# One order for the recurrence: a hand-written order on five engines, second buffers, pair sums between chain steps, and loads in another order

## The chip, the cores and the metric

The kernel runs on one core of one Trainium2 chip. The time is device microseconds (us) of one execution, as the median of several runs. The engines are PE (TensorE matmul, its weight loads shown as PEld), DVE (VectorE), ACT (ScalarE), POOL (GpSimd) and SP (SyncE, which here only issues DMAs).

## The reference, cut to what matters

A two-layer trunk for 1024 tokens of width 1024, in float32. Layer 1 mixes tokens with a gated linear recurrence (HGRN2, 8 heads of 128), layer 2 with windowed attention; each layer ends with a gated feed-forward part. The change lies in the first mixer and in what is loaded and prepared beside it:

```python
q, f, i, g = split(h @ w_in, 4)                # 1024 x 4096 weights, 8 heads of 128
fg = lb + (1 - lb) * sigmoid(f)                # the decay, per token and channel
# S_t = diag(fg_t) S_{t-1} + (1 - fg_t) i_t^T ;  o_t = S_t^T silu(q_t), in chunks
o = hgrn2_chunkwise(silu(q), 1 - fg, i, log(fg))
o = o * rsqrt(mean(o^2) + eps) * g_norm_w * silu(g)
mix = o @ w_out
h = layer_norm(ALPHA * h + mix)                # then the feed-forward part, layer 2, ...
```

## The kernel before, in words

**Matmuls in three products.** Each large product is done with both operands split in a high and a low part: ACT casts the high part, DVE subtracts to get the low part (`split_raw`, `split`: ACT line L151 or L196, DVE line L144), and PE does three matmuls for each pair of tiles (`mm3`, lines L169, L170, L171). Weights arrive in three `raw` buffers (`raw_tail`) and are split into a ring `HL` of six tiles.

**The recurrence stage**, about the first 515 us, walks heads 0 to 7 in *slots*, stretches of projection matmuls. Each head has four slots of `qf` (f and q projections by halves of 512 tokens; ACT makes sigmoid, `fg`, and `kp` = 1 − fg; DVE multiplies `qs`) and four slots of `ig_block` (value and gate projections of two token blocks; ACT writes `V` at L684 and `G` at L685, DVE multiplies `G` at L686). Around each slot, `slot_begin` issues loads and stores on SP and `slot_end` makes the weight splits for the next head and, in some slots, four *pair sums* (L999 to L1002): differences of quarter blocks of the second feed-forward weights, which are loaded into the free tiles of `Y`, summed and stored to memory for later.

**The chain** of a head is the task `recur(h)`. It is spawned at slot `lead[h]` of the `ig_block` slots (lead 3 for head 1, 2 for heads 2 to 5, 1 for heads 6 and 7) and interleaved with the slots' matmuls: every `yield n` lets about n us of other matmuls go first, counted by modelled matmul costs in `od.t`. Its steps, for one head:

- DVE: `r0` (tile `St`, L858), `qp` (L859), `r1` (tile `kd`, L861), `update(0)` (qp L848, kp L850, tot L853), and two products `r2` (tile `og`, L865). This is called the r-chain below.
- PE: column sums of r0, r1, r2 (L175, `psax<-St,one`, `<-kd,one`, `<-og,one`), then `update(1)` (qp and tot on DVE, kp on POOL) and four masked copies into `Ab` (L828).
- for i = 2 to 6: PE `scores` (`psax<-qp,kp`), then `update(i)` and a copy: each step's scores need the previous step's `update`.
- PE transposes, ACT copies `kd`; then state products, `St` on DVE, output products, `og`, and at the end transposes of `og`.

**Who sets the order.** In before only PE and SP have the source's order in this stage (`manual_schedule` with PE and SP). On ACT, DVE and POOL a scheduler places each instruction where its own costs say, with the splits and the pair sums held behind two anchors (`issue_after`). After head 7 the output projection begins (`out_part`), which needs `T` filled from `Y` (`Y_to_T`, lines L196 and L144) and `w_out` loaded and split. Convolution parameters (`conv_params`) are loaded by ACT's DMA queue, transposed on PE (L769), late in this stage.

Of the kernel before, what the change touches and what calls it, by code (L numbers as in the profile page):

```python
# [87 lines left out]
def trunk(ctx: ExitStack, tc: tile.TileContext, a: dict, out: bass.AP):  # L88
# [574 lines left out]
    with tc.tile_pool(name="t", bufs=1, reuse_waits="tile") as raws, hgrn_pool as hp:  # L663
# [9 lines left out]

        VG = {}

        def ig_block(h, us, tp):
            if tp == 0:
                VG[h] = (hp.tile([P, NB, P], F32, name="V"), hp.tile([P, NB, P], F32, name="G"))
            V, G = VG[h]
            ps = psmm()  # L680
            proj_tok(us, tp, ps)
            pv = ps.rearrange("p (t g c) -> p t g c", t=2, g=2)
            ts = slice(2 * tp, 2 * tp + 2)
            nc.scalar.copy(V[:, ts, :], pv[:, :, 0, :])  # L684
            act = nc.scalar.activation(G[:, ts, :], pv[:, :, 1, :], AF.Sigmoid)  # L685
            return act, nc.vector.tensor_tensor(G[:, ts, :], G[:, ts, :], pv[:, :, 1, :], op=ALU.mult)  # L686
# [10 lines left out]
        with tc.tile_pool(name="ep", bufs=1, reuse_waits="tile") as ep:  # L697
            pr = ep.tile([81, P], F32, name="pr")

            def x_load(tb):  # L700
                nc.sync.dma_start(Y[:, tb, :], x[tb * P:(tb + 1) * P, :])

            def x_block(tb):
                ps = psax()
                for kc in range(KC):
                    tr(ps[:, kc * P:(kc + 1) * P], Y[:, tb, kc * P:(kc + 1) * P])
                ts = slice(tb * P, (tb + 1) * P)
                split(T[:, 0, :, ts], T[:, 1, :, ts], ps.rearrange("p (k t) -> p k t", k=KC))
# [8 lines left out]
            nc.scalar.copy(warm, nhalf)  # L717
            with tc.manual_schedule(engines={EN.PE, EN.SP, EN.Activation, EN.DVE}):
                x_load(0)
# [21 lines left out]
            mf = hp.tile([P, 7 * BL + P], F32, name="kd")  # L741
            nc.sync.dma_start(mf, a["masks"])
# [12 lines left out]
            nc.vector.tensor_tensor(lbt[:, 0, :], le[:, 0, :], lm, op=ALU.mult)  # L755
            nc.vector.tensor_scalar(lbt[:, 1, :], lbt[:, 0, :], -1.0, 1.0, op0=ALU.mult, op1=ALU.add)
            ig_block(0, us, NB // 2 - 1)

        def conv_params():
            yield 360.0  # L760
            for l in range(2):
                for k in range(2):
                    cr = hp.tile([88, P], F32, name="cr", bufs=2)
                    for j in range(2):
                        q = 2 * k + j
                        src = a["ffn_conv_w"][l, q] if q < 3 else a["ffn_conv_b"][l]
                        nc.scalar.dma_start(cr[44 * j:44 * (j + 1), :], src.rearrange("(c p) -> c p", p=P))
# [4 lines left out]
                    yield 0.0  # L772
# [5 lines left out]
            yield 0.0  # L778
# [3 lines left out]
            nc.vector.tensor_copy(rl, ps[:16, :2 * P])  # L782
            nc.scalar.dma_start(rbd, rl.unsqueeze(1).to_broadcast([16, P, 2 * P]))

        params = od.spawn(conv_params())

        def qf_load(h, g):
            wv = w_in.rearrange("(kc p) c -> p kc c", p=P)
            c0 = g * D + h * P
            return load(lambda r: [(r.rearrange("p (k c) -> p k c", k=KC), wv[:, :, c0:c0 + P])])  # L790

        def qf_split(raw):
            return split_raw(raw).rearrange("p h (k c) -> p h k c", k=KC)

        def qf(h, weights):
# [3 lines left out]
            kp = hp.tile([P, S], F32, name="kp")  # L799
            for half in range(2):  # L800
# [4 lines left out]
                act = nc.scalar.activation(fg[:, ts], fg[:, ts], AF.Identity, bias=lbt[:, 0, h:h + 1],  # L805
                                           scale=lbt[:, 1, h:h + 1])
                nc.scalar.activation(kp[:, ts], fg[:, ts], AF.Identity, bias=one[:, 0:1], scale=-1.0)
                yield act, None
                ps = psmm()
                proj_T(weights["q"], half, ps)  # L810
                act = nc.scalar.activation(qs[:, ts], ps, AF.Sigmoid)
                yield act, nc.vector.tensor_tensor(qs[:, ts], qs[:, ts], ps, op=ALU.mult)
            weights["out"] = qs, fg, kp

        def recur(h, qs, fg, kp):
# [65 lines left out]
            for i in range(2, 7):  # L881
# [19 lines left out]
                put()  # L901
                if i == 4:
# [60 lines left out]
        busy = {s for c in begins for s in (c, c + 1)}  # L963
        free, loads, sums, stores = {r: 0 for r in (0, 2, 4, 6)}, {}, {}, {}
        for i in range(2 * pairs):
            for s in range(8 * NH):
                for r in free:
                    at = next(n for n in range(s + 2, 9 * NH) if n not in busy and n not in sums)
                    if s not in loads and free[r] <= s and at + 1 <= begins[r] + 4:
                        break  # L970
# [3 lines left out]
            loads[s], sums[at], stores[at + 1], free[r] = (i, r), (i, r), (i, r), at + 2  # L974
        slot_no = [-1]
        anchor = {}

        def slot_begin():
# [5 lines left out]
            if n in loads:  # L984
                i, r = loads[n]
                for k in range(2):
                    row = (k * pairs + i % pairs) * P
                    nc.sync.dma_start(Y[:, r + k, :], a["ffn_w_out"][i // pairs][row:row + P, :])

        def slot_end(act, dve, *makes):  # L990
            anchor["act"], anchor["dve"] = act, dve or anchor.get("dve", act)
            with tc.issue_after(anchor["act"].ins), tc.issue_after(anchor["dve"].ins):
                for make in makes:
                    make()
                if slot_no[0] in sums:
                    r = sums[slot_no[0]][1]
                    blocks = Y[:, r:r + 2, :].rearrange("p a (b n) -> p a b n", b=2)
                    (b11, b12), (b21, b22) = [(blocks[:, k, 0], blocks[:, k, 1]) for k in range(2)]
                    tt(b11, b12, b11, op=sub)  # L999
                    tt(b12, b22, b12, op=sub)  # L1000
                    tt(b22, b22, b11, op=sub)
                    tt(b21, b21, b22, op=sub)  # L1002

        values_done = [-1]
        with tc.manual_schedule(engines={EN.PE, EN.SP}):
            w = {g: qf_split(qf_load(0, k)) for k, g in enumerate("qf")}
# [3 lines left out]
            for k in range(4):  # L1010
                slot_begin()
                slot_end(*next(steps), *(make_w[k - 1:k] if k else ()))
# [4 lines left out]
            for h in range(1, NH):  # L1017
# [4 lines left out]
                for make in ((), make_ig[:1], make_ig[1:], ()):  # L1022
                    slot_begin()
                    slot_end(*next(steps), *make)
# [5 lines left out]
                else:  # L1030
                    make_w = []
                for tp in range(NB // 2):
# [4 lines left out]
                    slot_end(*ig_block(h, us, tp), *(make_w[tp - 1:tp] if tp else ()))  # L1037
                w = nw
        od.finish([params])
        wo = a["hgrn_w_out"][0]  # L1040
        rows1 = lambda k: [(0, P, wo[k * P:(k + 1) * P, :])]
# [3 lines left out]
        us = []  # L1045
        for u in range(4):
            us += out_unit(rows1, u)
# [345 lines left out]
```

## Time and profile before

| | us |
|---|---|
| median of 3 runs | 2214.83 (2211.97 to 2215.96) |
| profiled execution, its own time | 2211.82 |
| its span, first to last instruction | 2209.8 |
| outside the span | 2.0 |
| mean granted PE clock | 0.997 |
| recurrence stage within the span | about 0 to 515 |

Of the span PE is busy 98%, DVE 80%, ACT 42%, POOL 8%. A row of a timeline reads: start, duration, engine, line, operation, output tile <- input tiles, shape, count; in brackets the idle time of the engine before it and what ended that. A row of the windows view lists a stretch, its length, busy time of each engine with instruction counts, the granted clock, the busy share of the DMA engines and GB/s. A row of the waits view lists the engine, the line that waited and for what, the total wait, how often, and the longest wait.

### The profile page before, as it was taken

The numbers are of one execution on the slowest core, as the hardware profiler recorded it, in microseconds if no ns is written. First come the engines' busy times: TensorE is split into PE (matmuls) and PEld (weight loads), VectorE is DVE, ScalarE is ACT, GpSimd is POOL, SyncE is SP. The second block draws the span as 40 slices with busy tenths as digits, with TensorE's granted clock in tenths as the row PEclk, the third lists the DMA queues.
The fourth block names the chain that finished last, engine by engine and source line by source line (L and its number), as shares of the span: only waits on it lengthen the run. The fifth ranks groups of instructions, "written<-read, shape, count | busy, mean of one in ns | idle before, by whom it ended". The sixth has DMA issues, their size and how long they took to land.

```text
span 2209.8 us, 33157 instructions
## 1 busy us (share of the span) xinstructions
PE 2168.1 (98%) x13007; PEld 1810.5 (82%) x13007; DVE 1777.6 (80%) x2415; ACT 932.1 (42%) x1601; POOL 178.6 (8%) x196
## 2 busy tenths in 40 slices
PE   8999999989999999999999999999999999999998
PEld 7888888878888888887888888878888888887887
DVE  2777665555789888988997779977899888889987
ACT  4333333332744334344343546655654444343431
POOL 0122111110100000000000013211000000000001
PEclk9999999999999999999999999999999999999999
DMA  6565443152223222227954431123123222249663
GB/s 197 173 208 195 161 168 120 48 97 89 96 69 104 86 86 86 86 79 252 303 162 153 106 99 35 34 81 120 67 96 105 80 73 77 86 153 315 202 208 137
DMA packets 231942, 281.14 MB, mean 127 GB/s; under 512 B 29977, under 2 KB 160746, under 8 KB 228970
## 3 DMA queue, kind: packets, MB, share of 16 engines
q1 hardware_dynamic: 228898, 276.57, 38.6%
q10 hardware_dynamic: 2888, 2.45, 0.9%
q8 instruction: 102, 1.67, 0.3%
q14 instruction: 54, 0.44, 0.1%
HBM read 213.96 MB, written 65.01 MB: 126 GB/s over the span
## 4 chain that ended last, share of the span: by engine, by line
PE 82%; DVE 9%; DMA 4%; ACT 3%; issue 2%; POOL 1%; SPq 0%; DVEq 0%; ACTq 0%; POOLq 0%
PE psmm L169 17%; PE psmm L171 17%; PE psmm L170 16%; PE psax L171 8%; PE psax L169 8%; PE psax L170 8%; PE psax L175 3%; DVE T L144 1%; PE psmm L175 1%; PE psax L1185 1%; PE psax L179 1%; DVE HL L144 1%; ACT Y L244 1%; DMA raw<-in_hgrn_w_out_dram 1%; DMA raw<-in_hgrn_w_in_dram 1%
## 5 line engine op out<-in xcount | busy, mean ns | idle before, releaser
L169 PE MATMUL psmm<-T,HL 128*128 128x512 f32 x768 | 307.1, 400 | 0.0
L170 PE MATMUL psmm<-T,HL 128*128 128x512 f32 x768 | 300.2, 391 | 2.1 <-DVE T L144 2.1
L171 PE MATMUL psmm<-T,HL 128*128 128x512 f32 x768 | 300.8, 392 | 0.0
L474 DVE SCALAR_TENSOR_TENSOR Y<-Y,cwt 128x1023 f32<-128x1023 f32 (+1 forms) x176 | 225.3, 1280 | 39.9 <-ACT Y L472 39.7
L472 ACT ACTIVATE Y<-Y,cwt 128x1024 f32<-128x1024 f32 x88 | 109.1, 1240 | 263.6 <-DVE Y L461 260.6
L169 PE MATMUL psmm<-HL,T 128*128 128x256 f32 (+1 forms) x656 | 201.0, 306 | 1.0 <-ACT T L196 1.0
L171 PE MATMUL psmm<-HL,T 128*128 128x256 f32 (+1 forms) x656 | 196.2, 299 | 2.0 <-DVE T L144 2.0
L170 PE MATMUL psmm<-HL,T 128*128 128x256 f32 (+1 forms) x656 | 196.3, 299 | 1.7 <-DVE HL L144 1.7
L196 ACT CAST HL<-rx 128x1024 fp32r<-128x1024 f32 (+1 forms) x137 | 140.3, 1045 | 122.4 <-DMA rx<-in_ffn_w_in_dram 33.3
L144 DVE TENSOR_TENSOR HL<-rx,HL 128x1024 fp32r<-128x1024 f32 (+1 forms) x137 | 165.9, 1213 | 12.3 <-ACT HL L196 12.0
L170 PEld LDWEIGHTS psmm<-T,HL 128*128 128x128 f32 x768 | 144.4, 188 | 31.3 <-DVE T L144 2.9
L169 PEld LDWEIGHTS psmm<-T,HL 128*128 128x128 f32 x768 | 144.3, 188 | 31.1 <-issue 1.2
L171 PEld LDWEIGHTS psmm<-T,HL 128*128 128x128 f32 x768 | 144.1, 188 | 31.0
L171 PE MATMUL psax<-T,HL 128*128 128x512 f32 x352 | 137.6, 391 | 0.0
L169 PE MATMUL psax<-T,HL 128*128 128x512 f32 x352 | 137.5, 391 | 0.0
L170 PE MATMUL psax<-T,HL 128*128 128x512 f32 x352 | 137.4, 390 | 0.0
L169 PEld LDWEIGHTS psmm<-HL,T 128*128 128x128 f32 x656 | 127.4, 194 | 7.8 <-issue 2.9
L171 PEld LDWEIGHTS psmm<-HL,T 128*128 128x128 f32 x656 | 127.2, 194 | 5.9 <-DVE T L144 2.7
L170 PEld LDWEIGHTS psmm<-HL,T 128*128 128x128 f32 x656 | 127.5, 194 | 5.4 <-DVE HL L144 2.1
L218 POOL TENSOR_TENSOR rs<-rs,nhalf 128x1 f32<-128x1 f32 x32 | 26.0, 813 | 1293.2 <-DVE rs L217 1292.9
L850 POOL TENSOR_TENSOR kp<-kp,tot 128x512 f32<-128x512 f32 x48 | 73.6, 1534 | 293.6 <-PE psax L175 151.7
L196 ACT CAST HT<-rx 128x1024 fp32r<-128x1024 f32 (+1 forms) x51 | 44.0, 863 | 89.4 <-PE psmm L170 30.5
(298 smaller groups left out, 5251.5 us busy)
## 6 DMA issues: line engine op xcount, KB each, us to landing
rx<-in_ffn_w_in_dram SPq DMA_DIRECT2D x136, 256.0 KB, 3.4
rx<-gd SPq DMA_DIRECT2D x118, 256.0 KB, 3.5
Y<-in_ffn_w_out_dram SPq DMA_DIRECT2D x44, 512.0 KB, 6.6
bsd<-Y SPq DMA_DIRECT2D x22, 1024.0 KB, 3.9
gd<-Y SPq DMA_DIRECT2D x44, 512.0 KB, 2.7
rx<-in_ffn_w_out_dram SPq DMA_DIRECT2D x54, 256.0 KB, 3.8
R<-bsd SPq DMA_DIRECT2D x44, 256.0 KB, 4.8
Y<-in_ffn_w_in_dram SPq DMA_DIRECT2D x40, 256.0 KB, 3.3
```

What stands on the lines that cost most here:

```text
L144: make = lambda e: e.tensor_tensor(lo, src, hi.bitcast(F32), op=ALU.subtract)
L169: nc.tensor.matmul(ps, st(0), mv(0), start=start, stop=False)
L170: nc.tensor.matmul(ps, st(0), mv(1), start=False, stop=False)
L171: nc.tensor.matmul(ps, st(1), mv(0), start=False, stop=stop)
L175: nc.tensor.matmul(ps, lhsT, rhs, start=start, stop=stop, **kw)
L179: nc.tensor.transpose(ps, src, ident)
L196: nc.scalar.copy(hi, src)
L218: nc.gpsimd.tensor_tensor(rs, rs, nhalf, op=ALU.pow)
L244: nc.scalar.activation(hf[:, kc, :], ps[:, k * P:(k + 1) * P], AF.Identity, bias=shift, scale=scale)
L472: nc.scalar.activation(c, u, AF.Identity, bias=cwt[:, l, 3, ci:ci + 1], scale=cwt[:, l, 2, ci:ci + 1])
L474: nc.vector.scalar_tensor_tensor(c[:, sh:], u[:, :S - sh], cwt[:, l, 2 - sh, ci:ci + 1], c[:, sh:], op0=ALU.mult, op1=ALU.add)
L850: (nc.gpsimd if i else nc.vector).tensor_tensor(kv[:, :, 0, :], kv[:, :, 0, :], tv[:, :, 1:2].to_broadcast([P, nb, m]), op=ALU.mult)
```

## The change

Line numbers of the kernel after are some 7 to 14 higher than before's in this part (L848 becomes L856, L865 becomes L873; the pair sums, L999 to L1002, all become L1013).

- `V`, `G` and `kp` get two buffers each. In `ig_block` the sigmoid now comes before the copy of `V`.
- The recurrence runs with the source's order on PE, SP, ACT, DVE and POOL. The anchors go; the splits stand at the end of a slot as written.
- The pair sums are put in a list in `slot_begin`, and taken from it by `between(n)`: four at a slot's end, two after each score step, four after the values. The slot kept free of them is one before the chain's first slot instead of the two after it. The store comes two slots after the sums instead of one.
- The largest score step (i = 6) uses blocks of 32 columns of `kp` instead of 64.
- Loads at the start: tokens 4 and 5, f weights, tokens 6 and 7, q weights, parameters, masks; before: parameters, tokens 4 to 7, masks, q, f. Convolution parameters are loaded ten units of matmul time ahead of their transposes.
- At the end of the stage three of the four `w_out` units are loaded at head 7 and split at the ends of its slots 1 to 3, instead of after all slots.

```diff
-                VG[h] = (hp.tile([P, NB, P], F32, name="V"), hp.tile([P, NB, P], F32, name="G"))
+                VG[h] = (hp.tile([P, NB, P], F32, name="V", bufs=2), hp.tile([P, NB, P], F32, name="G", bufs=2))
...
+            nc.scalar.activation(G[:, ts, :], pv[:, :, 1, :], AF.Sigmoid)
             nc.scalar.copy(V[:, ts, :], pv[:, :, 0, :])
-            act = nc.scalar.activation(G[:, ts, :], pv[:, :, 1, :], AF.Sigmoid)
-            return act, nc.vector.tensor_tensor(G[:, ts, :], G[:, ts, :], pv[:, :, 1, :], op=ALU.mult)
+            nc.vector.tensor_tensor(G[:, ts, :], G[:, ts, :], pv[:, :, 1, :], op=ALU.mult)
...
+                for tb in range(4, 6):
+                    x_load(tb)
+                rawf = qf_load(0, 1)
+                for tb in range(6, NB):
+                    x_load(tb)
+                rawq = qf_load(0, 0)
...
-                for tb in range(4, NB):
-                    x_load(tb)
+                nc.sync.dma_start(mf, a["masks"])
...
-            kp = hp.tile([P, S], F32, name="kp")
+            kp = hp.tile([P, S], F32, name="kp", bufs=2)
...
                         for b in range(P // (2 * m)):
-                            o = 2 * m * b
-                            mm32(ps[o:o + m, c * P + o + m:c * P + o + 2 * m],
-                                 kp[:, c * P + o:c * P + o + m],
-                                 qp[:, c * P + o + m:c * P + o + 2 * m], cost=0.056 * m / 32,
-                                 tile_position=(0, o))
+                            t = c * P + 2 * m * b + m
+                            for o in range(2 * m * b, 2 * m * b + m, BL):
+                                mm32(ps[o:o + BL, t:t + m], kp[:, c * P + o:c * P + o + BL], qp[:, t:t + m],
+                                     cost=0.03 * m / BL, tile_position=(0, o))
...
                 update(i)
                 put()
+                between(2)
...
             nc.vector.tensor_tensor(og, pv, G, op=ALU.mult)
+            values_done[0] = h
+            between(4)
+            yield 5.0
             nc.vector.tensor_tensor(og, og, ss.unsqueeze(2).to_broadcast([P, NB, P]), op=ALU.mult)
-            values_done[0] = h
-            yield 8.0
+            yield 3.0
...
-        busy = {s for c in begins for s in (c, c + 1)}
+        busy = {s for c in begins for s in (c - 1,)}
...
-            loads[s], sums[at], stores[at + 1], free[r] = (i, r), (i, r), (i, r), at + 2
+            loads[s], sums[at], stores[at + 2], free[r] = (i, r), (i, r), (i, r), at + 3
...
+        def between(n):
+            while pending and n:
+                pending.pop(0)()
+                n -= 1
...
-        def slot_end(act, dve, *makes):
-            anchor["act"], anchor["dve"] = act, dve or anchor.get("dve", act)
-            with tc.issue_after(anchor["act"].ins), tc.issue_after(anchor["dve"].ins):
-                for make in makes:
-                    make()
...
+        def slot_end(*makes):
+            for make in makes:
+                make()
+            between(4)
...
-        with tc.manual_schedule(engines={EN.PE, EN.SP}):
-            w = {g: qf_split(qf_load(0, k)) for k, g in enumerate("qf")}
+        with tc.manual_schedule(engines={EN.PE, EN.SP, EN.Activation, EN.DVE, EN.Pool}):
+            w = {g: qf_split(raw) for g, raw in (("f", rawf), ("q", rawq))}
...
-                    make_w = []
+                    oraw = [load(out_loads(rows1, 0, (2 * u, 2 * u + 1))) for u in range(3)]
+                    make_w = [lambda u=u: out_split(oraw[u]) for u in range(3)]
...
-        us = []
-        for u in range(4):
-            us += out_unit(rows1, u)
+        out_split(load(out_loads(rows1, 0, (6, 7))))
+        us = out_us
```

More of the change, by code (lines that the diff above doesn't have):

```diff
@@ L672, in ig_split, with qf_load, qf_split @@
             return split_raw(raw, eng).rearrange("p h (k c) -> p h k c", k=4)
+        def qf_load(h, g):
+            c0 = g * D + h * P
+            return load(lambda r: [(r.rearrange("p (k c) -> p k c", k=KC), w_iv[:, :, c0:c0 + P])])
+        def qf_split(raw):
+            return split_raw(raw).rearrange("p h (k c) -> p h k c", k=KC)
         VG = {}
@@ L716, in trunk @@
             warm = sm.tile([P, 1], F32, name="warm")
-            nc.scalar.copy(warm, nhalf)
+            mf = hp.tile([P, 7 * BL + P], F32, name="kd")
             with tc.manual_schedule(engines={EN.PE, EN.SP, EN.Activation, EN.DVE}):
+                nc.scalar.copy(warm, nhalf)
                 x_load(0)
@@ L761, in conv_params @@
             for l in range(2):
+                crs = []
                 for k in range(2):
-                    cr = hp.tile([88, P], F32, name="cr", bufs=2)
+                    crs.append(hp.tile([88, P], F32, name="cr", bufs=2))
                     for j in range(2):
@@ L766, in conv_params @@
                         src = a["ffn_conv_w"][l, q] if q < 3 else a["ffn_conv_b"][l]
-                        nc.scalar.dma_start(cr[44 * j:44 * (j + 1), :], src.rearrange("(c p) -> c p", p=P))
+                        nc.scalar.dma_start(crs[k][44 * j:44 * (j + 1), :], src.rearrange("(c p) -> c p", p=P))
+                yield 10.0
+                for k, cr in enumerate(crs):
                     ps = psmm()
@@ L777, in conv_params @@
             nc.scalar.dma_start(oh, a["onehot"])
-            yield 0.0
+            yield 10.0
             ps = psmm()
@@ L782, in conv_params @@
             nc.vector.tensor_copy(rl, ps[:16, :2 * P])
+            yield 3.0
             nc.scalar.dma_start(rbd, rl.unsqueeze(1).to_broadcast([16, P, 2 * P]))
         params = od.spawn(conv_params())
[L787 to L793, printed above, removed]
         def qf(h, weights):
@@ L968, in trunk @@
                     at = next(n for n in range(s + 2, 9 * NH) if n not in busy and n not in sums)
-                    if s not in loads and free[r] <= s and at + 1 <= begins[r] + 4:
+                    if s not in loads and free[r] <= s and at + 2 <= begins[r] + 5:
                         break
@@ L973, in trunk @@
                 break
-            loads[s], sums[at], stores[at + 1], free[r] = (i, r), (i, r), (i, r), at + 2
+            else:
+                raise ValueError("no slot for a unit")
+            loads[s], sums[at], stores[at + 2], free[r] = (i, r), (i, r), (i, r), at + 3
         slot_no = [-1]
-        anchor = {}
+        pending = []
+        def between(n):
+            while pending and n:
+                pending.pop(0)()
+                n -= 1
         def slot_begin():
@@ L988, in slot_begin, with out_split @@
                     nc.sync.dma_start(Y[:, r + k, :], a["ffn_w_out"][i // pairs][row:row + P, :])
-        def slot_end(act, dve, *makes):
-            anchor["act"], anchor["dve"] = act, dve or anchor.get("dve", act)
-            with tc.issue_after(anchor["act"].ins), tc.issue_after(anchor["dve"].ins):
-                for make in makes:
-                    make()
[L995 to L1002, printed above, removed]
-        values_done = [-1]
-        with tc.manual_schedule(engines={EN.PE, EN.SP}):
-            w = {g: qf_split(qf_load(0, k)) for k, g in enumerate("qf")}
+            if n in sums:
+                r = sums[n][1]
+                blocks = Y[:, r:r + 2, :].rearrange("p a (b n) -> p a b n", b=2)
+                (b11, b12), (b21, b22) = [(blocks[:, k, 0], blocks[:, k, 1]) for k in range(2)]
+                for x, y, z in ((b11, b12, b11), (b12, b22, b12), (b22, b22, b11), (b21, b21, b22)):
+                    pending.append(lambda x=x, y=y, z=z: tt(x, y, z, op=sub))
+        def slot_end(*makes):
+            for make in makes:
+                make()
+            between(4)
+        values_done = [-1]
+        wo = a["hgrn_w_out"][0]
+        rows1 = lambda k: [(0, P, wo[k * P:(k + 1) * P, :])]
+        out_us = []
+        def out_split(raw):
+            hl = split_raw(raw)
+            out_us.extend([hl[:, :, :512], hl[:, :, 512:]])
+        with tc.manual_schedule(engines={EN.PE, EN.SP, EN.Activation, EN.DVE, EN.Pool}):
+            w = {g: qf_split(raw) for g, raw in (("f", rawf), ("q", rawq))}
             nw, nraw = {}, {g: qf_load(1, k) for k, g in ((1, "f"), (0, "q"))}
@@ L1011, in trunk @@
                 slot_begin()
-                slot_end(*next(steps), *(make_w[k - 1:k] if k else ()))
+                next(steps)
+                slot_end(*(make_w[k - 1:k] if k else ()))
             for _ in steps:
@@ L1023, in trunk @@
                     slot_begin()
-                    slot_end(*next(steps), *make)
+                    next(steps)
+                    slot_end(*make)
                 for _ in steps:
@@ L1036, in trunk @@
                     slot_begin()
-                    slot_end(*ig_block(h, us, tp), *(make_w[tp - 1:tp] if tp else ()))
+                    ig_block(h, us, tp)
+                    slot_end(*(make_w[tp - 1:tp] if tp else ()))
                 w = nw
         od.finish([params])
-        wo = a["hgrn_w_out"][0]
-        rows1 = lambda k: [(0, P, wo[k * P:(k + 1) * P, :])]
         for half in range(2):
```

15 lines of the change are left out of this document (7 added, 8 removed).

## The prediction, on record before the kernel ran

> **What bounds it now.** I read the page first, then the windows by stage, then what PE waited for in the stage that the change touches.
>
> ```profile
> PE 2168.1 (98%) x13007; PEld 1810.5 (82%) x13007; DVE 1777.6 (80%) x2415; ACT 932.1 (42%) x1601; POOL 178.6 (8%) x196
> PE 82%; DVE 9%; DMA 4%; ACT 3%; issue 2%; POOL 1%; SPq 0%; DVEq 0%; ACTq 0%; POOLq 0%
> 0.00:12.00 12.00, 5.47 (x24) 5.06 (x25) 1.71 (x2) 4.96 (x6) 4.38 (x11) 1.00 0.86 262
> 12.00:40.00 28.00, 24.97 (x208) 24.36 (x207) 13.56 (x19) 13.18 (x18) 0.00 (x0) 1.00 0.82 276
> 40.00:440.00 400.00, 396.05 (x4158) 349.71 (x4158) 255.56 (x413) 130.15 (x297) 75.09 (x54) 1.00 0.44 147
> 440.00:515.00 75.00, 68.70 (x646) 60.16 (x645) 36.05 (x55) 24.33 (x58) 11.75 (x8) 0.93 0.44 93
> ```
>
> PE is busy 98% of the span and carries 82% of the chain. The PE work is the same in both kernels except for one score step, so the change can only move idle time and granted clock. From 40 to 440 us PE stands idle under 4 us of 400: the middle of the recurrence has almost nothing to give, and much to lose. The end of the stage, 440 to 515, is where idle time (6.3 us) and a low clock (0.93) are. Behind 515 the order of all engines is unchanged, and I let it cost nothing.
>
> The waits of PE, first for 40 to 440 (five rows), then 440 to 515 (three), then 12 to 40 (three):
>
> ```profile
> PE psax L175 <- DVE og L865: 1.5, 1, 1.5
> PE psax L175 <- DVE qp L848: 1.3, 1, 1.3
> PE psmm L769 <- DMA cr<-in_ffn_conv_w_dram: 0.5, 1, 0.5
> PE psax L175 <- issue: 0.3, 1, 0.3
> PE psax L175 <- ACT kd L913: 0.3, 1, 0.3
> ...
> PE psax L175 <- DVE og L865: 3.7, 1, 3.7
> PE psax L175 <- DVE qp L848: 1.9, 1, 1.9
> PE psmm L170 <- DVE HL L144: 0.6, 1, 0.6
> ...
> PE psmm L170 <- DVE HL L144: 1.1, 1, 1.1
> PE psmm L169 <- ACT T L196: 1.0, 1, 1.0
> PE psmm L171 <- DVE T L144: 1.0, 1, 1.0
> ```
>
> So the middle has 3.9 us of waits, the end 6.2, the start 3.1. Behind the two long waits at the end the clock was halved, here in windows cut at its edges:
>
> ```profile
> 472.90:479.80 6.90, 5.35 (x28) 4.54 (x29) 6.90 (x9) 4.39 (x8) 2.13 (x1) 0.51 0.00 0
> 486.60:490.03 3.43, 3.43 (x19) 3.43 (x18) 2.97 (x4) 2.94 (x3) 1.33 (x1) 0.50 0.04 8
> ```
>
> At half clock PE does half the work: 5.35/2 and 3.43/2, so 2.7 + 1.7 = 4.4 us more are lost.
>
> **Middle: the r-chain comes late.** Head 3 stands for all. DVE, ACT and PE before:
>
> ```profile
> 220.27 1.23 DVE L858 TENSOR_TENSOR St<-qs,kp 128x1024 f32<-128x1024 f32 x1
> 224.60 1.29 DVE L865 TENSOR_TENSOR og<-kp,qp 128x512 f32<-128x512 f32 x2
> 225.93 0.69 DVE L848 TENSOR_TENSOR qp<-qp,tot 128x512 f32<-128x512 f32 x1
> 231.92 0.42 DVE L686 TENSOR_TENSOR G<-G,psmm 128x256 f32<-128x256 f32 x1 [4.97 <-ACT G L685]
> 232.26 0.69 DVE L999 TENSOR_TENSOR Y<-Y 128x512 f32<-128x512 f32 x1
> 232.86 1.22 DVE L144 TENSOR_TENSOR HL<-raw,HL 128x1024 fp32r<-128x1024 f32 x1
> 234.00 0.69 DVE L1000 TENSOR_TENSOR Y<-Y 128x512 f32<-128x512 f32 x1
> 234.72 0.69 DVE L1001 TENSOR_TENSOR Y<-Y 128x512 f32<-128x512 f32 x1
> 231.77 1.05 ACT L151 CAST HL<-raw 128x1024 fp32r<-128x1024 f32 x1
> 238.27 0.61 PE L175 MATMUL psax<-og,one 128*32 128x256 f32 x8
> 241.52 0.76 PE L175 MATMUL psax<-qp,kp 128*32 128x32 f32 x64
> L853 DVE TENSOR_TENSOR tot<-fg x7: 686/693/698, 61.3 to 385.7; 128x512 f32<-128x512 f32 x7
> ```
>
> Before, the scheduler ran the r-chain and even the first update (qp at 225.93) some 11 us before PE took the sums at 238.27. After, DVE has the source's order. Set side by side, the instruction orders show for heads 1 to 5: G of slot lead−1, the low part of a weight split, then r0, qp, r1, qp, kp, tot, r2 twice. The low part waits for ACT's cast, which stands behind that slot's G and V and so still ends at about 232.8; the low part keeps its 232.86 and frees DVE at 234.00 (next row's start). The chain takes 225.93 − 220.27 = 5.66 us, and about 0.6 more for the tot that before did elsewhere (693 ns, less the overlap of starts). So r2 is ready at 234.00 + 5.66 + 0.6 = 240.26, and PE, whose own order puts the r2 sums at 238.27, waits 2.0 us. While PE waits, every projection matmul behind it in PE's order waits too. Five heads: **+10.0**.
>
> Next the update before the first scores. Before had it done at 226.6. After, DVE's order has behind r2: G (0.34 by the starts 231.92, 232.26), a low part (1.14), four pair sums (0.60 by the starts 232.26 and 232.86, 0.72 twice by 234.00 and 234.72, 0.69 for the last: 2.73), then qp: 240.26 + 0.34 + 1.14 + 2.73 + 0.69 = 245.16. PE's scores, moved by the first wait, are due at 241.52 + 2.0 = 243.5: a second wait of 1.6. This is the case in heads 2, 3, 4 (+4.8). Head 1 has no low part there (+0.5). Head 5 has no sums there (nothing: 242.4 against 243.5). Head 6 has no low part ahead of its r-chain, so r2 comes 0.3 late, then the same queue (+1.9). Together **+7.2**; the bound from below is nothing, should the sums stand elsewhere than the orders show, from above 2.7 more for head 5.
>
> What goes: head 0's wait of 1.5 I halve, since its chain too gets splits and sums before it (−0.75). The qp, cr, issue and kd waits (1.3 + 0.5 + 0.3 + 0.3) go with the second `kp`, the earlier loads and the free V buffer. **−3.1**. The second buffers can give no more, for there is no more wait.
>
> The score step with 32 columns:
>
> ```profile
> L175 PE MATMUL psax<-qp,kp 128*64 128x64 f32 x112 | 8.0, 225 | 1.3 <-DVE qp L848 1.3
> ```
>
> 8.0/7 = 1.15 us a head for 16 records; the 64 records of 32 columns at 241.52 took 0.76. Twice as many, half as wide: I take no change, with 0.4 a head either way as ends (±2.7).
>
> **Clock.** A wait of 1.9 us at the end was followed by 3.43 us at half clock, waits of 1.5 and 1.3 in the middle by none (window 40 to 440, clock 1.00). The new waits are 2.0 (five) and 1.6 (four), astride that. Each half window costs 1.7; I take two, **+3.4** (ends 0 and 15.3). The Trainium skill ("TensorE: Matmul & The Clock Gate", HAM oscillation) has a rule of no PE-idle gaps over about 3.4 us; by it none of these waits would cost clock and the sum would be 3.4 less. The trace goes against it with its 0.50 after a gap of 1.9.
>
> **End.**
>
> ```profile
> 471.13 1.05 ACT L151 CAST HL<-raw 128x1024 fp32r<-128x1024 f32 x1 [14.78 <-DMA raw<-in_hgrn_w_out_dram]
> 472.62 2.94 ACT L196 CAST T<-Y 128x1024 fp32r<-128x1024 f32 x3
> 472.77 0.42 DVE L686 TENSOR_TENSOR G<-G,psmm 128x256 f32<-128x256 f32 x1 [10.82 <-ACT G L685]
> 477.25 3.48 DVE L144 TENSOR_TENSOR T<-Y,T 128x1024 fp32r<-128x1024 f32 x3
> ```
>
> Before, ACT stood 14.8 us at a cast whose `w_out` data was late, DVE's G and r2 behind it, and PE's sums behind these. After, `w_out` is loaded during head 7 and the cast stands later: this wait goes, with its 3.7, the 1.9, the 0.6 and 4.4 of clock, 10.6 in all. In exchange the orders show between r2 and the third step's scores on DVE: two G, four parts of T (3.48 for three, some 0.6 for a half one), two low parts, and qp, tot and the masked copies (estimated 2.7 together), 9.8 us, where PE gives about 6.2 (sums to scores 3.25 by head 3; to the next scores 2.2 of other matmuls by the code and 0.76); less what DVE does before the sums, that is 0.6 to 3.6 late, I take 2.5. And the last low part before the output projection stands on ACT and DVE behind T casts, copies to A and G and V of the last slot: 0 to 4.5, I take 3.5. Two such waits, two half windows: 3.4. So 9.4 come back: **−1.2** (−10.6 to +3).
>
> **Start.**
>
> ```profile
> 20.16 0.37 ACT L684 COPY V<-psmm 128x256 f32<-128x256 f32 x1 [1.14 <-PE psmm L171]
> ```
>
> The T waits (2.0) go, since the weight splits no longer stand before the last T splits. But the f split now precedes the T splits of tokens 2 and 3. Nine loads of 0.52 MB up to f: 3.1 MB by 12 us at 262 GB/s, the rest at 276 in 5.7, so f lands at about 17.7; its cast (1.05), a T cast (0.98 as at 472.62) and a low part (1.16 as at 477.25) put the first of these T parts at 20.9 and the second at 22, where PE had done its first block (V at 20.16) and goes on: +1.5. **−0.5** (−2 to +3).
>
> **Sum.** 10.0 + 7.2 − 3.1 + 3.4 − 1.2 − 0.5 = +15.8 on the profiled execution's 2211.8: 2227.6. That execution lies 3 us under the median and at the low end of the runs, so I say 2228.
>
> **Rivals.**
> *Faster: DVE keeps ahead of PE.* Place: DVE's queue in slots lead−1 and lead. If DVE came through it 2.0 us sooner by the r2 sums and 3.6 sooner by the scores than the rows of head 3 add up to, PE would meet both steps ready, and the 17.2 and the 3.4 vanish: 2211.8 − 3.1 − 1.2 − 0.5 = 2207, or 2198 if the end gives all it has. For it: DVE is only 64% busy in the middle (255.56 of 400), the added r-chain position is not in any trace, and before held such waits to two. Against it: the orders are fixed, and the low part cannot begin before ACT's cast ends at 232.8. 0.19.
> *Half clock behind every new wait.* Nine windows at 1.7 instead of two: 2228 + 11.9 = 2240. For it: 2.0 exceeds the 1.9 that was enough. Against: 1.5 was not, and four are 1.6. 0.13.
> *Nothing moves.* The new waits and what is gained at both ends (10.6 and 2.0) balance: 2212. It needs the end at its best and half the middle waits. 0.08.
> *The forecast*, 2216.5 to 2235: 0.60.
>
> **Range and chances.** About 4.4 us (0.2%) is what a measurement of this kernel can tell from no change; its runs spread over 4. The range takes in the half clock above and reaches to the faster case below: 2207 to 2240. Faster 0.19, same 0.08, slower 0.73.
>
> **What would show it.** In the trace after: PE waits for `og` (L873) at the column sums in heads 1 to 5 of about 2.0 each, and for `qp` (L856) of about 1.6 in heads 2, 3, 4 and 6; r0 starting on DVE right after a low part; window 40 to 440 with PE idle about 15 us more; no 14.8 us idle on ACT near 456. Wrong it is if the middle shows no `og` waits, or if the end shows waits well above 6 us.

## The result

| | before | after |
|---|---|---|
| median, us | 2215.39 (2211.97 to 2216.02, 4 runs) | 2241.06 (2239.16 to 2242.96, 4 runs) |
| profiled execution: span, us | 2209.8 | 2238.3 |
| mean granted PE clock | 0.997 | 0.995 |

The kernel after takes 1.0119 times as long (95% interval 1.0102 to 1.0137): 25.7 us more. Slower was forecast, at 2228, with a range up to 2240. The forecast's sum of 15.8 started from the profiled execution of before, which lay some 3 us under the median; from one profiled span to the other the loss is 28.5 us.

**Where it went.** PE's order is nearly the same in both kernels, so the start of the same matmul can be compared in both traces. The r2 column sums (`psax<-og,one`) and the first matmul of the output projection serve as posts:

| post on PE | before, us | after, us | behind by |
|---|---|---|---|
| r2 sums of head 0 | 74.36 | 72.89 | −1.5 |
| head 1 | 126.26 | 134.92 | +8.7 |
| head 2 | 180.38 | 191.62 | +11.2 |
| head 3 | 238.27 | 255.82 | +17.6 |
| head 4 | 296.16 | 320.13 | +24.0 |
| head 5 | 354.56 | 383.75 | +29.2 |
| head 6 | 406.69 | 436.08 | +29.4 |
| head 7 | 474.45 | 501.76 | +27.3 |
| first `psax` matmul behind the recurrence | 518.33 | 546.92 | +28.6 |

Behind the recurrence nothing more is lost: 28.6 there and 28.5 in the span. By stages the loss is: start −1.0; head 0 +7.7; head 1 +2.6; heads 2, 3, 4 +6.3, +6.4, +5.2; head 5 +2.0; head 6 +2.1; head 7 and the end −2.7. Each stage runs from the first column sums (`psax<-St,one`) of one head to those of the next, which stand just ahead of the wait for r2; the start ends at those of head 0. (At head 7's r2 post before itself had waited 3.7 us, so the table shows after less behind there than the stages add up to.)

### The profile page after: what moved, and what is told of

Its sections match the earlier page's. It is cut to its first block, busy times and chain, and to the rows that moved or that the text cites. A ratio compares the mean times of both kernels' runs of the same rounds, so it can differ in the third digit from the quotient of the medians.

```text
span 2238.3 us, 33375 instructions
## 1 busy us (share of the span) xinstructions
PE 2173.8 (97%) x13135; PEld 1814.8 (81%) x13135; DVE 1790.2 (80%) x2415; ACT 931.9 (42%) x1601; POOL 171.6 (8%) x196
## 4 chain that ended last, share of the span: by engine, by line
PE 74%; DVE 15%; ACT 4%; DMA 3%; issue 3%; POOL 1%; SPq 1%; DVEq 0%; ACTq 0%; POOLq 0%
PE psmm L169 15%; PE psmm L171 15%; PE psmm L170 15%; PE psax L171 8%; PE psax L169 8%; PE psax L170 8%; PE psax L175 3%; DVE HL L144 2%; DVE T L144 2%; DVE Y L1013 1%; DMA rx<-in_ffn_w_in_dram 1%; PE psmm L175 1%; PE psax L179 1%; PE psax L1210 1%; DVE Y L474 1%
## 5 line engine op out<-in xcount | busy, mean ns | idle before, releaser
L169 PEld LDWEIGHTS psmm<-HL,T 128*128 128x128 f32 x656 | 129.2, 197 | 8.5 <-issue 3.0
L170 PEld LDWEIGHTS psmm<-HL,T 128*128 128x128 f32 x656 | 129.0, 197 | 5.4 <-DVE HL L144 2.2
L171 PEld LDWEIGHTS psmm<-HL,T 128*128 128x128 f32 x656 | 128.8, 196 | 5.1 <-DVE T L144 1.9
L144 DVE TENSOR_TENSOR HL<-raw,HL 128x1024 fp32r<-128x1024 f32 x51 | 67.8, 1329 | 41.4 <-ACT HL L151 40.6
L858 POOL TENSOR_TENSOR kp<-kp,tot 128x512 f32<-128x512 f32 x48 | 66.8, 1392 | 328.8 <-DVE og L873 197.2
```

The source lines that it names most:

```text
L144: make = lambda e: e.tensor_tensor(lo, src, hi.bitcast(F32), op=ALU.subtract)
L169: nc.tensor.matmul(ps, st(0), mv(0), start=start, stop=False)
L170: nc.tensor.matmul(ps, st(0), mv(1), start=False, stop=False)
L171: nc.tensor.matmul(ps, st(1), mv(0), start=False, stop=stop)
L858: (nc.gpsimd if i else nc.vector).tensor_tensor(kv[:, :, 0, :], kv[:, :, 0, :], tv[:, :, 1:2].to_broadcast([P, nb, m]), op=ALU.mult)
```

## The profile after

The page's first and fourth part, and the windows of the two later stages (columns as before: busy time by engine, clock, DMA share, GB/s):

```profile
PE 2173.8 (97%) x13135; PEld 1814.8 (81%) x13135; DVE 1790.2 (80%) x2415; ACT 931.9 (42%) x1601; POOL 171.6 (8%) x196
PE 74%; DVE 15%; ACT 4%; DMA 3%; issue 3%; POOL 1%; SPq 1%; DVEq 0%; ACTq 0%; POOLq 0%
...
40.00:440.00 400.00, 374.03 (x3840) 328.45 (x3838) 246.67 (x373) 119.36 (x278) 62.68 (x49) 0.98 0.40 134
440.00:515.00 75.00, 69.24 (x827) 63.00 (x828) 46.01 (x72) 27.55 (x56) 13.34 (x10) 0.98 0.22 67
```

DVE's share of the chain rose from 9% to 15%. From 40 to 440 us PE was idle for 26.0 us instead of 4.0, and its clock was 0.98 instead of 1.00. The waits of PE from 40 to 440, and from 440 to 530:

```profile
PE psax L175 <- DVE og L873: 10.2, 6, 1.8
PE psax L175 <- DVE qp L856: 6.9, 5, 2.6
PE psax L175 <- DVE tot L861: 5.5, 3, 3.2
PE psax L175 <- issue: 1.6, 1, 1.6
PE psmm L170 <- issue: 1.0, 1, 1.0
...
PE psax L175 <- DVE qp L856: 4.7, 2, 2.6
PE psax L175 <- issue: 1.6, 1, 1.6
PE psmm L169 <- ACT HL L151: 1.6, 1, 1.6
PE psmm L170 <- DVE HL L144: 0.9, 1, 0.9
```

Five of the six `og` waits are the forecast ones; the sixth, of 1.1 us, is head 0's. Those for `tot` were not forecast. DVE's timeline in head 3, and POOL's kp, PE's column sums and PE's first scores beside it:

```profile
248.41 1.23 DVE L144 TENSOR_TENSOR HL<-raw,HL 128x1024 fp32r<-128x1024 f32 x1 [0.52 <-ACT HL L151]
249.56 1.22 DVE L866 TENSOR_TENSOR St<-qs,kp 128x1024 f32<-128x1024 f32 x1
254.48 1.28 DVE L873 TENSOR_TENSOR og<-kp,qp 128x512 f32<-128x512 f32 x2
255.69 0.42 DVE L693 TENSOR_TENSOR G<-G,psmm 128x256 f32<-128x256 f32 x1
256.02 2.21 DVE L144 TENSOR_TENSOR HL<-raw,HL 128x1024 fp32r<-128x1024 f32 x1
258.15 2.85 DVE L1013 TENSOR_TENSOR Y<-Y 128x512 f32<-128x512 f32 x4
260.92 0.68 DVE L856 TENSOR_TENSOR qp<-qp,tot 128x512 f32<-128x512 f32 x1
...
255.85 1.30 POOL L858 TENSOR_TENSOR kp<-kp,tot 128x512 f32<-128x512 f32 x1 [22.07 <-DVE og L873]
255.82 0.79 PE L175 MATMUL psax<-og,one 128*32 128x256 f32 x8 [1.81 <-DVE og L873]
261.75 0.33 PE L175 MATMUL psax<-qp,kp 128*32 128x32 f32 x17 [1.09 <-DVE qp L856]
```

This is the queue as the prediction worked it out: low part, r-chain, G, low part, sums, qp. From the low part's end to r2's end it took 6.1 us (249.56 to 255.69; worked out were 6.26), and from there to qp's start 5.2 (worked out 4.2). The extra 1.0 is in one row: the low part at 256.02, which lies beside POOL's kp, took 2.21 us, not 1.22.

## The experiments

The theory at this point (A): the loss comes from the source's order on DVE and ACT, which puts splits and sums ahead of the chain. The rival (B): it comes from the other edits. Ratios are against runs of before on the same chip. Differences from after are differences of medians that may come from two chips; before's medians lay between 2213.5 and 2215.4 us.

**Order taken back.** After, with DVE, ACT and POOL left to the scheduler:

```diff
-        with tc.manual_schedule(engines={EN.PE, EN.SP, EN.Activation, EN.DVE, EN.Pool}):
+        with tc.manual_schedule(engines={EN.PE, EN.SP}):
...
+            with tc.issue_after(anchor["act"].ins), tc.issue_after(anchor["dve"].ins):
+                for make in makes:
```

> The kernel after with one thing taken back: ACT, DVE and POOL are placed by the scheduler again (splits and pair sums held behind the last ACT and DVE instruction of their slot, as in before); buffers, loads, slots of the pair sums, the 32-column score step stay. Theory A (the loss is the source's order on DVE and ACT): the og and qp waits in the middle go, and what the ends gained stays: 2205 to 2214 us. Rival B (the loss comes from the other edits: where the sums are put, the narrower score step, the loads): it stays at 2230 or above.

Measured: 2209.09 us, 0.9977 of before (0.9967 to 0.9988). PE idle from 40 to 440 went from 26.0 to 8.7 us, and no half clock is left in the recurrence:

```profile
40.00:440.00 400.00, 391.29 (x4233) 345.35 (x4233) 243.92 (x402) 127.39 (x294) 74.39 (x54) 1.00 0.42 142
440.00:515.00 75.00, 74.10 (x715) 65.09 (x715) 43.58 (x63) 27.83 (x68) 12.78 (x10) 1.00 0.43 111
```

A stands: without the order the rest of the change is a small gain.

**Order alone.** Before, with the second buffers and the source's order on all five engines:

> The kernel before with only the source's order on all five engines in the recurrence, and the second buffers for V, G and kp. Theory A: slower than before by 20 us or more, with PE waits for r2 (og) of about 2 us in heads 1 to 5. Rival B: within 5 us of before.

Measured: 2268.94 us, 1.0248 (1.0233 to 1.0263). PE waited for r2 (`og`) 15.4 us in six places from 40 to 440, the longest 2.7. So the order costs 54 us with before's code in it. The rest is by difference: the other edits of the change (sums between the steps and in other slots, w_out earlier, rbd later) win back about half of that; under this order they were not taken apart. B falls.

**The r-chain moved.** After, with each chain spawned one slot earlier:

```diff
-            yield 8.0 if h == NH - 1 else 5.0
+            yield (8.0 if h == NH - 1 else 5.0) + (6.1 if h else 0.0)
...
-                    if tp == lead[h]:
+                    if tp == lead[h] - 1:
```

> The kernel after, with the task of each head from 1 on spawned one slot earlier and its column sums delayed by one slot (6.1 us of matmuls), so that on DVE the r-chain stands before the weight split of slot lead-1; PE's order stays nearly as it is. Theory A1 (place in the order): the five og waits of 2.0 us go, and with them the half clock windows that follow two of them: about 2228 us. Rival A2 (DVE's queue as a whole is too long between the sums and the scores): what PE gains at the sums it waits more at the first scores, 2236 to 2241.

Measured: 2232.2 us, 1.0082 (1.0067 to 1.0097), between the two expectations. All five r2 waits went, but PE got a new one, for the head before, which the earlier spawn makes the kernel finish at once (its last `og` product stands just ahead of PE's transposes):

```profile
PE psax L179 <- DVE og L954: 11.6, 3, 4.6
PE psax L175 <- DVE tot L861: 5.8, 4, 3.2
PE psax L175 <- DVE qp L856: 3.7, 5, 0.9
```

**And the first slot's sums moved** behind the chain's first update. (Before keeps the chain's first slot and the next one free of sums; after keeps only the slot ahead of the first, so four sums stand at the first slot's end.)

```diff
                 make()
-            between(4)
+            if slot_no[0] not in begins:
+                between(4)
```

> The chain one slot earlier, and besides no pair sums at the end of the slot in which the chain's sums stand (they go between the later score steps). Theory A1: the waits at the first scores go as well (1.25 to 2.75 us in heads 2, 3, 4, 6): 2217 to 2224 us, with head 0's 8 us still there. Rival A2: the sums then delay a later score step, and it stays above 2228.

Measured: 2233.49 us, no better; the rival, above 2228, had the number. From 40 to 440 PE's waits for `qp`, 3.7 us in the run before, are gone, but those for `tot`, in later score steps, rose from 5.8 to 10.0, all of them before 220 us: there the moved sums do delay a later step. The new wait for the head before stands as it was, in heads 1, 2 and 6, where the head before was not yet through. From 220 to 405 us only 0.7 us of waits are left. So both edits were made once more in heads 3, 4 and 5 alone.

> The kernel after with the chain one slot earlier in heads 3, 4 and 5 alone (where the head before is through by then, so that nothing of it is hurried), and the pair sums of those heads' first slot moved between the score steps. Theory A1: from the column sums of head 3 to those of head 6 the kernel loses nothing against before any more; 6.3 + 5.3 + 2.0 = 13.6 us of the loss go, about 2227 us. Rival A2 (DVE's queue as a whole): less than half of it comes back, above 2234.

Measured: 2228.93 us, 1.0063 (1.0045 to 1.008), 12.1 us less than after. The waits view of PE has no row at all from 254 to 420 us; after had 8.4 us of waits (og, qp, issue) from 253 to 382. From the sums of head 3 to those of head 6 this kernel gains 1.4 us on before, where after loses 13.6. (Its head 2 takes 1.3 us longer than after's, so most of the 1.4 may be matmuls that moved across that post.) The place in DVE's order is the cause there, both of the first and of the second wait, and DVE's queue as a whole is not too long.

**Head 0's 8 us.** First guess: the sums between its steps.

```diff
                 put()
-                between(2)
```

> The kernel after without pair sums between the score steps (they stay in the list until a slot's end or the values). Theory A3 (head 0's loss of 8 us is a circle: sums between the steps make DVE late for Ab, ACT's copies of Ab wait for it in ACT's order, fg and the weight cast stand behind these, DVE's low part behind the cast, qp behind the low part): head 0 loses 3 us or less, about 2236 us. Rival: head 0 is late from the four sums ahead of its first update alone, and nothing is gained, 2239 to 2243.

Measured: 2245.93 us, 1.0144 (1.0128 to 1.0159): worse by 5 us. The sums then stood four in a row at the slots' ends, ahead of the next update. This theory fell. The timelines of the kernel after, ACT's first, showed another:

```profile
89.78 1.65 ACT L913 COPY A<-Ab 32x256 f32<-32x256 f32 x4 [8.51 <-DVE Ab L836]
91.45 0.60 ACT L811 ACTIVATE fg<-psmm 128x512 f32<-128x512 f32 x1
93.56 1.03 ACT L151 CAST HL<-raw 128x1024 fp32r<-128x1024 f32 x1
...
94.62 1.23 DVE L144 TENSOR_TENSOR HL<-raw,HL 128x1024 fp32r<-128x1024 f32 x1 [3.57 <-ACT HL L151]
95.76 0.68 DVE L856 TENSOR_TENSOR qp<-qp,tot 128x512 f32<-128x512 f32 x1
...
96.59 1.92 PE L175 MATMUL psax<-qp,kp 128*32 128x64 f32 x32 [3.16 <-DVE tot L861]
```

ACT stood 8.5 us at copies that wait for DVE's Ab; the sigmoid of f and the weight cast stood behind them in ACT's order; DVE's low part waited 3.6 us for the cast, qp behind it, and PE's scores 3.2 us behind that. The copies are needed only at the head's last products, so they can be issued after the last score step:

```diff
-                if i == 4:
+                if i == 6:
                     for b in range(P // BL):
```

> The kernel after with ACT's four copies A<-Ab issued after the last score step instead of after step i = 4. Theory A4 (the cross wait of head 0 runs through ACT's order: copies wait for Ab, the sigmoid of f and the weight cast stand behind the copies, DVE's low part behind the cast, qp behind it): PE's wait of 3.3 us before the first i = 6 scores of head 0 and the two half clock windows behind it go, and the last low part of w_out comes about 1.6 us earlier: 2232 to 2236 us. Rival: DVE's own queue is what is late there; the wait stays within 1 us, 2239 to 2242.

Measured: 2232.93 us, 1.0093 (1.0077 to 1.0109), 8.1 us less than after. PE's waits for `tot` from 40 to 440 fell from 5.5 to 1.8 us, and in the traces head 0 got back 5.5 of its 7.7 us. The cross wait through ACT was the cause of about 3 us of wait there and of two windows at half clock. What the other 2.2 us of head 0 are was not tested.

**Both repairs together.**

> Source order on all engines, repaired where the waits were found: chain one slot earlier in heads 3, 4, 5, their first sums later, copies A<-Ab late. If the places in the order add up: 2228.9 less what the late copies bring (5 to 7 us): 2222 to 2224 us. Rival: the late copies only move the waits: 2227 or above.

Measured: 2220.91 us, 1.0034 (1.0019 to 1.0049). The two gains (12.1 and 8.1) add up: 20.2 of the 25.7 us. From 245 to 400 us no wait of PE is left; those that remain stand in heads 0, 1, 2 and 6. That is no proof that a written order costs nothing: the run with the order taken back, which has the change's other edits too, took 2209.09 us, 12 less.

**POOL beside DVE.** kp updated on DVE instead of POOL:

```diff
-                (nc.gpsimd if i else nc.vector).tensor_tensor(kv[:, :, 0, :], kv[:, :, 0, :],
+                nc.vector.tensor_tensor(kv[:, :, 0, :], kv[:, :, 0, :],
```

> The kernel after with all kp updates on DVE instead of POOL. Theory C (a DVE operation that lies beside POOL's kp is held up by about 1.0 us, as the low part of 2.21 us instead of 1.22 at 256 us was): DVE's work per head grows by 5 times 0.6 us and loses up to 5 times 1.0 us; DVE operations in the recurrence all come to their usual lengths, and the time stays within 5 us of after. Rival: the long DVE operations have another cause (waits inside them for data): they stay long, and the time rises by the added 0.6 us a step, 10 us or more.

Measured: 2237.35 us, 1.0105 (1.008 to 1.0129), 3.7 less than after; with two runs, and an interval that overlaps after's, that is no clear gain, but the rise of 10 us or more that the rival asked for is not there. The groups of DVE from 40 to 450 us, after first, then this kernel:

```profile
L144 DVE TENSOR_TENSOR HL<-raw,HL 128x1024 fp32r<-128x1024 f32 x26 | 37.3, 1435 | 28.9 <-ACT HL L151 28.2 <-DMA Y<-in_ffn_w_out_dram 0.6
L861 DVE TENSOR_TENSOR tot<-tot 128x8 f32<-128x8 f32 x6 | 6.1, 1014 | 0.0
L861 DVE TENSOR_TENSOR tot<-tot 128x64 f32<-128x64 f32 x7 | 6.1, 868 | 0.0
...
L144 DVE TENSOR_TENSOR HL<-raw,HL 128x1024 fp32r<-128x1024 f32 x26 | 31.8, 1223 | 29.1 <-ACT HL L151 28.7 <-DMA Y<-in_ffn_w_out_dram 0.4
L861 DVE TENSOR_TENSOR tot<-tot 128x8 f32<-128x8 f32 x6 | 1.0, 160 | 0.0
L861 DVE TENSOR_TENSOR tot<-tot 128x64 f32<-128x64 f32 x7 | 1.5, 218 | 0.0
L858 DVE TENSOR_TENSOR kp<-kp,tot 128x512 f32<-128x512 f32 x39 | 26.6, 683 | 0.0
```

A `tot` of 8 columns took 1014 ns beside POOL's kp and 160 without it. In before it was 167: there the scheduler had worked out `tot` ahead, away from kp (in head 7, where it did meet kp, it took 1.12 us). Theory C holds: DVE is held up by the kp beside it. All that DVE does for kp itself, 26.6 us, is about what it lost beside POOL's.

**The end, and a faster version.** What does the change hold besides the order? First, with the scheduler and with before's slots, places and stores for the sums:

> What the change has besides the order: the kernel after with the scheduler on ACT, DVE and POOL, and with before's slots, stores and places for the pair sums; second buffers, loads, the narrow score step and the early w_out remain. Theory A: before less 1 us at the start, 7 us at the end and 2 us in the middle: 2203 to 2207 us. Rival: the early w_out and the loads gain only where the sums are also moved: within 2 us of the run with the scheduler and moved sums, 2209.

Measured: 2203.15 us, 0.9954 (0.9937 to 0.9971): faster than before. Then w_out late again in that version:

```diff
-                    make_w = [lambda u=u: out_split(oraw[u]) for u in range(3)]
+                    make_w = []
...
```

> The fastest version so far (scheduler on ACT, DVE, POOL, before's pair sums; 2203 us) with w_out loaded and split after all slots again, as in before. Theory: the end's gain of 7.6 us is the early w_out alone: 2209 to 2212 us, with ACT idle again near 455 us and og waits and half clock behind it. Rival: it is the convolution parameters' earlier loads, or the later bias copy: 2203 to 2206 us.

Measured: 2200.16 us, 0.9946 (0.9927 to 0.9965). My theory fell: the end gains with w_out loaded late too. The traces showed what differs: the broadcast write `rbd` of the convolution task, 2 MB from one small tile. In before it was issued at 444.73 and landed at 469.74; the w_out load issued at 456.10 had landed by 471.06. In this version it was issued at 481.49, when the loads were through. Two runs put it to the test. Only the convolution task of after, in before:

```diff
+                yield 10.0
+                for k, cr in enumerate(crs):
...
-                    yield 0.0
+                    yield 3.0
...
-            yield 0.0
+            yield 10.0
...
+            yield 3.0
             nc.scalar.dma_start(rbd, rl.unsqueeze(1).to_broadcast([16, P, 2 * P]))
```

> The kernel before with only the task of the convolution parameters as in after: its loads stand ahead of the transposes, and the broadcast write rbd comes some 25 us of matmul time later. Theory D (the wait of 14.8 us for w_out in before was made by the rbd write on the DMA engines, 444.7 to 469.7 us, in the way of the load issued at 456.1): ACT's wait at the w_out cast goes and with it the og and qp waits and the half clock of the end, 2203 to 2207 us. Rival (w_out is slow for another cause, such as its place behind the split it waits for): 2211 to 2216.

Measured: 2202.49 us, 0.9956 (0.9939 to 0.9972). And the task of before in the 2200 us version:

> The version with the scheduler, before's pair sums and w_out loaded after all slots (2200 us), with the convolution task of before, that is with rbd early again. Theory D: the end's gain goes again, 2207 to 2212 us. Rival: 2199 to 2203.

Measured: 2212.83 us, 0.9994 (0.9982 to 1.0007). ACT's timeline, first of before with after's convolution task, then of the fast version with before's; and last, from before, the DMA queues in 455 to 472 us (q10 carries `rbd`, q1 the loads; packets, MB, share of the 16 engines):

```profile
444.71 1.05 ACT L151 CAST HL<-raw 128x1024 fp32r<-128x1024 f32 x1 [2.40 <-DMA raw<-in_hgrn_w_out_dram]
482.29 0.66 ACTq L787 DMA_DIRECT2D rbd<-rl  x1
...
447.36 0.66 ACTq L795 DMA_DIRECT2D rbd<-rl  x1
474.04 1.05 ACT L151 CAST HL<-raw 128x1024 fp32r<-128x1024 f32 x1 [15.74 <-DMA raw<-in_hgrn_w_out_dram]
...
q10 hardware_dynamic: 1247, 1.26, 67.3%
q1 hardware_dynamic: 288, 0.52, 8.0%
```

Moved from both sides, the `rbd` write takes the long wait for w_out with it. (The edit also moves the task's small `cr` loads and transposes. That the write is the cause rests on the queues: the load got 8% of the DMA engines' time while `rbd` had 67%, and it landed 1.3 us after `rbd` had.) That one edit is worth 11.4 us; the other edits of the fast version add no more than the 2.3 us between 2202.49 and 2200.16, whose intervals overlap.

**Second buffers alone**, in before:

> The kernel before with second buffers for V, G and kp and nothing else; PE's order is unchanged. By the waits of before (kd 0.3, issue 0.3, qp 1.3) it gains 0 to 2 us: 2212 to 2215 us. Rival: the scheduler uses the freedom to run further ahead, and more of the middle's 3.9 us of waits goes, or new ones come: outside 2210 to 2217.

Measured: 2213.01 us, 0.9998 (0.9987 to 1.0009): nothing that can be measured. By the code the source's order needs them (with one V, the next head's V would stand ahead of the products that still read the old one); this was not run without them. They bring no time.

## Why the prediction came out as it did

- **First waits: right.** Forecast were 2.0 us in each of heads 1 to 5. Against before, PE lost 2.0 at the r2 sums of each of these five (8.66 − 6.65 in head 1, and so on; the waits view says 1.8).
- **Second waits: right in kind, short in size.** Forecast were 1.6 in heads 2, 3, 4 and 6. Counted as PE's lost time between two matmul starts they were 2.75, 1.25, 1.25 and 2.76; head 1, with 0.5 forecast, has 1.2 in the waits view. The term lacked POOL's kp beside the low part: 1.0 us there, and as much beside `tot` in later steps. That heads 3 and 4 came out under 1.6 is not the forecast's merit: a half clock window begins just behind their r2 sums (256.19 and 321.04), so PE itself came to the scores up to 1.7 us later.
- **Head 0: wrong, and the largest miss.** It was to gain 0.75; it lost 7.7. That is some 8.5 of the 12.7 us between the sum's 15.8 and the 28.5 from span to span. The step that failed was "head 0's wait of 1.5 I halve". I had looked at DVE's order alone. ACT's order joins in: the copies of Ab ahead of the cast (shown by moving them: 5.5 us back in head 0, 8.1 over the whole kernel).
- **Later score steps: not in the sum.** Heads 3, 4 and 6 lost another 1.2 to 1.8 in one place each, booked as "issue". 16 KB of instructions were being fetched beside two of them (265.08 and 448.43, PE resumed at 267.46 and 450.98). That the fetch is the cause was not tested, and 31 such fetches stand in 40 to 450 us, most of them beside no such gap.
- **Half clock: the term was too small.** Two windows were taken (3.4 us); from 40 to 440 there were five (95.76 to 102.59 for two, then from 198.16, 256.19 and 321.04), and one more at 512.18. At half clock each costs up to 1.7 us, so up to 8.5 in the middle. By the rule of the Trainium skill ("TensorE: Matmul & The Clock Gate", HAM oscillation) only gaps over some 3.4 us cost clock. The trace goes against it here too: gaps of 1.8 us halved it.
- **The rival "half clock behind every new wait"** named 2240, the nearest number, and that is luck. Of its nine windows three came (behind the first waits of heads 3 and 4 and the second of head 2); two more stand in head 0, of which it had nothing.
- **End: size near, cause wrong.** Forecast −1.2, measured −2.7. The long wait on ACT went as said, but w_out loaded earlier is not needed for that: it is enough that the `rbd` write no longer lies beside the load (two runs). Whether early w_out with `rbd` early would have done it too was not run. The `rbd` write is not in the prediction, so that the wait went is in part luck. What came back was near the terms: 2.3 us for the qp of the third step's scores (2.5 taken), 2.9 for the last low part (3.5 taken), one half clock window (two taken).
- **Start: −1.0 against −0.5.** The waits for T fell from 2.0 to 0.3, and the f split in front of them cost little.
- **The faster rival** was given 0.19. It would have needed DVE ahead of PE; that came only with the scheduler back.

## What to carry to other kernels

Where an engine's order is written by hand, walk every engine's queue, not only the one on the critical path: a copy that may come late, put early on ACT, held up DVE and PE by a circle. Before a scheduler is replaced, read what it does ahead of time (here the r-chain 11 us early, and `tot`); source order gives that up unless the source is written so. And when a load is late, look first at what else is on the DMA engines: moving one broadcast write brought 11 us, with one small edit.

## What the runs showed of the hardware

**The clock follows idle time in fixed windows.** In each trace the stretches of half clock begin and end on a grid of 3.41 us. Two nearly equal waits (1.81 and 1.83 us) in the kernel after, in windows cut on that grid, the first in head 3, the second in head 1:

```profile
252.77:256.19 3.42, 1.61 (x28) 0.83 (x27) 3.42 (x7) 1.37 (x3) 0.34 (x1) 1.00 0.01 4
256.19:259.60 3.41, 3.41 (x22) 3.06 (x15) 3.34 (x4) 0.00 (x0) 0.95 (x1) 0.50 0.00 0
...
133.30:136.72 3.42, 1.80 (x13) 1.21 (x14) 3.42 (x5) 0.00 (x0) 1.31 (x1) 1.00 0.00 0
136.72:140.13 3.41, 2.18 (x54) 1.55 (x54) 3.31 (x7) 0.00 (x0) 0.00 (x0) 1.00 0.09 38
```

In head 3 the whole wait lay in one window (1.81 idle of 3.42), and the next window ran at 0.50. In head 1 it lay across the edge (1.62 idle in the second window), and the clock stayed. Over the fifteen kernels here that show half clock (the one with the order taken back shows none to lay the grid by), in 40 to 620 us: of 2385 full-clock windows with less than 1.65 us of idle PE none was followed by half clock, of 43 with 1.85 or more all were, of the 20 between 14 were. So about half a window of idle time decides, and a wait of 2 us costs either nothing more or another 1.7, by where it falls.

**POOL's tensor operations hold up DVE.** Small DVE operations beside a POOL operation of 1.1 to 1.6 us took about 1 us (1014 ns, and 160 with kp moved off POOL), and a low part 2.2 instead of 1.2.

**A broadcast write slows loads beside it.** With 2 MB of `rbd` in flight for 25 us, a w_out load took 15 us from issue to landing; with `rbd` elsewhere such a load landed in about 3 (issued at 449.83, landed at 452.86, in the 2200 us version).
